# First stage of a hybrid decoder layer: all loads on one queue, the casts behind the third root, a chunk turned a quad earlier

## The chip, the core and the metric

The kernel runs on one core of a Trainium2 chip. The metric is the device time of one execution in microseconds; the median of several runs stands for a kernel. Times inside the kernel come from one profiled execution.

## The reference

One layer of a decoder trunk on 16 meta tokens and 1024 real ones, width 1024, all float32:

```
h = concat(meta, x)
h = h + 1/2 * SwiGLU_1(RMSNorm(h))          # D_FF = 2816
u = RMSNorm(h) @ W_in
o = concat[HGRN2(u), StickBreaking(u)]      # parallel head groups
h = h + o @ W_out
h = h + 1/2 * SwiGLU_2(RMSNorm(h))
return h without the meta tokens

rms_norm(x, g) = x * rsqrt(mean(x*x) + 1e-6) * g
swiglu(h, w_in, w_out): g, u = split(h @ w_in); (silu(g) * u) @ w_out
```

## The kernel before

Every matrix product is made of three matmuls with float32 operands split in a high part (a cast, `wh` or `xh`) and a rest (`wl`, `xl`): high times high, rest times high, high times rest. The high part of a weight block is cast on ScalarE (L277, ACT in the profile) and its rest subtracted on VectorE (L279, DVE). Each split pair has three buffers.

The change is in the first stage, the first product of SwiGLU_1, in `run` and `fast_in`. The 1040 tokens are split in three chunks, `THIRDS`: chunk 0 of 352 tokens, chunks 1 and 2 of 344. Each chunk is loaded as three tiles of up to 128 rows of 1024 floats (`rows_of`, `load_rows`), from HBM as it lies. `norm_rows` makes the norm of each tile: a square with a sum (L648 on ScalarE for the first and third tile, L644 on VectorE for the second), a root (L649, ScalarE), a reciprocal (L650) and a scaling of the rows (L651), both on VectorE. `turned` transposes a chunk on TensorE (L631). For chunk 0 the results are evicted with the gain and split at once into `X` (L660 on ScalarE, L661 on VectorE). For chunk 2 they become `ba` and the operands B11 and B21 (`first_block`, L673 and `halve`, L222 and L223), for chunk 1 `bb`. `first_combined` then makes the operands T2, T3, T1, T4 and B22 from `ba` and `bb` in five groups of four steps.

Chunk 0 is multiplied plainly: `plain_quad` takes four weight blocks of 128 x 512 floats (two columns blocks of 128 by two halves of the depth), 12 matmuls each, 48 in all, in bank `qd`. Six such quads (gate and up of three pairs of columns) come first; they are the work beside which chunks 2 and 1 are normed, turned and combined. Chunks 1 and 2 are then multiplied together by a scheme with seven products of half blocks in place of eight (`quad`, banks `qa`, `qb`, `qc`), in which POOL (GpSimd) makes sums of weight blocks (L292). The other columns of chunk 0 are done along with it. Raw weight blocks (`raw`, L284) are loaded on SP's queue, 256 KB each.

The order of TensorE's instructions is that of the program. The other engines and the queues are put in order by a planner, from the program's order as priority and its own estimates of time; once built, each engine works through its own order strictly. Within the first stage the program's order is: chunk 0 normed and turned (at high priority), quad 1 (`next(steps)`), chunk 2 normed, quad 2, chunk 1 normed, chunk 2 turned, quads 3 and 4, chunk 1 turned, four steps of `first_combined` and quad 5, four steps and quad 6, the other twelve steps, and the combined quads. `setup_rest` (masks and small constants for later stages, L99 to L130) stands behind the plain quads and is moved forward by the planner where an engine is free.

The loads of chunk 0 stand on SP's queue, those of chunks 2 and 1 on POOL's, which in the profile is q0 (software_dynamic); SP's is q1.

Of the kernel before, what the change touches and what calls it, by code (L numbers as in the profile page):

```python
# [11 lines left out]
F32 = mybir.dt.float32  # L12
# [3 lines left out]
AF = mybir.ActivationFunctionType  # L16
# [4 lines left out]
P = 128  # L21
D = 1024
# [12 lines left out]
def drain(gen):  # L35
    for _ in gen:
        pass


class Block:  # L40
# [221 lines left out]
    def fast_in(self, ops, n, w_in, actD, openers, ev0, open_ev, feed=None, plain=None,  # L262
# [6 lines left out]
        nc = self.nc  # L269
        wp, pin = self.wq, self.pin  # L270
# [9 lines left out]
            return hi, lo  # L280

        def block(i, h, col):
            t = wp.tile([P, 4, P], F32, tag="raw", name="raw", bufs=6)
            nc.sync.dma_start(  # L284
                t, w_in[512 * h : 512 * h + 512, col + P * i : col + P * i + P]
                .rearrange("(k p) f -> p k f", p=P)
            )
            return t
# [6 lines left out]
        def weights(col, opened, also):  # L295
            if opened:
                yield operand(block(0, 0, col))
                yield operand(block(0, 1, col))
            a11, a21, a22, a12 = (
                block(i, h, col) for i, h in ((0, 0), (1, 0), (1, 1), (0, 1))  # L300
            )
            if opened is None:
                yield operand(a11)
            s1 = made(a21, nc.gpsimd.tensor_add, a22)
            s2 = made(s1, nc.gpsimd.tensor_sub, a11)
            yield operand(s2)
            if opened is None:
                yield operand(a12)
            yield operand(made(a11, nc.gpsimd.tensor_sub, a21))
            yield operand(s1)  # L310
            yield operand(a22)
            yield operand(made(a12, nc.gpsimd.tensor_sub, s2))
            if also:
                yield operand(a21)
# [323 lines left out]
    def norm_rows(self, ci, rows, junk):  # L638

        nc = self.nc  # L640
        for i, (row, at, m) in enumerate(rows):
            s, r = self.ss[:m, 3 * ci + i, 0:1], self.ss[:m, 3 * ci + i, 1:2]
            if i == 1:
                nc.vector.scalar_tensor_tensor(  # L644
                    junk[1][:m], row[:m], 1.0, row[:m], ALU.mult, ALU.mult, accum_out=s
                )
            else:
                nc.scalar.activation(junk[0][:m], row[:m], AF.Square, accum_out=s)  # L648
            nc.scalar.activation(r, s, AF.Sqrt, bias=self.eps[:m], scale=1.0 / D)  # L649
            nc.vector.reciprocal(r, r)  # L650
            nc.vector.tensor_scalar_mul(row[:m], row[:m], r)  # L651

# [673 lines left out]
    def run(self):  # L1326
        nc, tc, a = self.nc, self.tc, self.a
# [19 lines left out]
        with ExitStack() as c0:  # L1347
            with ExitStack() as c1:
                with tc.manual_schedule(engines={nc.tensor.engine}), ExitStack() as c2:
                    xo = self.pool("x_ops", ctx=c2)  # L1350
                    plain = [xo.tile([P, KT, n0], F32R, name=f"X0{i}") for i in range(2)]
                    ops = {
                        x: [xo.tile([P, 4, nw], F32R, name=f"{x}{i}") for i in range(2)]
                        for x in names
                    }
                    self.wq = self.pool("w1", ctx=c2)
                    ev0 = self.pool("ev10", ctx=c2)
                    self.pin = self.pool("pin1", 1, PSUM, c2)
                    self.t_bufs = 2
                    c3 = ExitStack()  # L1360
                    rp = self.pool("rows", ctx=c3, side="right")
                    junk = [rp.tile([P, D], (BF16, U8)[i], name=f"junk{i}") for i in range(2)]
                    self.row_bufs = 9
                    rows = [self.rows_of(0, rp, nc.sync)]
                    rows += [self.rows_of(ci, rp, nc.gpsimd) for ci in (2, 1)]
                    turning = []

                    def open_ev():
                        self.setup_rest(rp)
                        c3.close()  # L1370
                        ev = self.pool("ev1", ctx=c2)
                        turning.append(self.turn_x(self.pool("turn", ctx=c2), xD))
                        return ev

                    def between():
                        next(turning[0], None)

                    steps = self.fast_in(
                        ops, nw, a["ffn1_w_in"][0], act1D, 3, ev0, open_ev, None, plain, between
                    )  # L1380
                    with tc.high_priority():
                        self.first_plain(rows[0], junk, plain)
                    next(steps)
                    self.norm_rows(2, rows[1], junk)
                    next(steps)
                    self.norm_rows(1, rows[2], junk)
                    ba = self.first_block(2, rows[1], rp, "ba", ops)
                    next(steps)
                    next(steps)
                    bb = self.first_block(1, rows[2], rp, "bb", None)  # L1390
                    made = self.first_combined(ba, bb, ops, rp, nw)
                    for _ in range(2):
                        for _ in range(4):
                            next(made)
                        next(steps)
                    drain(made)
                    drain(steps)
                    drain(turning[0])
# [170 lines left out]
            with tc.manual_schedule(engines={nc.tensor.engine}), ExitStack() as cx:  # L1569
                with ExitStack() as c1:  # L1570
# [58 lines left out]
                    for i in summed(1, cB):  # L1629
                        if i == 4:  # L1630
                            r = self.inv_rms_rows(sums[0], n, px, pps)
                        if i == 7:
                            r = self.spread_rows(r, n, px, pps)
# [5 lines left out]
                operands(xb, ("T2", "T3", "T1", "T4", "B22"))  # L1639
                self.wq = self.pool("wq", ctx=cx)  # L1640
                self.pin = self.pool("pin2", 1, PSUM, cx)
                self.t_bufs = 2
                ppb = self.pool("ppb", 1, PSUM, pre)

                def open_ev():
# [8 lines left out]
                steps = self.fast_in(ops, n, a["ffn2_w_in"][0], actD, 2, ev0, open_ev, made)  # L1654
                r = self.inv_rms_rows(sums[1], n, px, ppb)
# [49 lines left out]
```

## Time and profile before

| | |
|---|---|
| runs | 2135.32, 2140.38, 2140.86 us (median 2140.38) |
| the profiled execution | 2136.56 us |
| its span | 2134.9 us |
| mean granted clock of TensorE | 0.988 |
| TensorE busy (matmul) | 2049.6 us, 96% |
| VectorE, ScalarE, POOL busy | 64%, 42%, 32% |
| first product of chunk 0 | 22.40 us after the span's start |
| first combined quad | 80.34 us |

The page gives the busy time of each engine, then its share in 40 slices of the span in tenths (9 is 90% or more). In the lists in order of time a row has the start and the length in us, the engine (PE is TensorE's matmul), the line, the operation, what it writes and reads, the shapes, and in brackets how long the engine stood idle before it and who released it. Matmuls overlap in the pipeline, so their lengths add up to more than the time they take.

### The profile page before, as it was taken

The numbers are of one execution on the slowest core, as the hardware profiler recorded it, in microseconds if no ns is written. First come the engines' busy times: TensorE is split into PE (matmuls) and PEld (weight loads), VectorE is DVE, ScalarE is ACT, GpSimd is POOL, SyncE is SP. The second block draws the span as 40 slices with busy tenths as digits, with TensorE's granted clock in tenths as the row PEclk, the third lists the DMA queues.
The fourth block names the chain that finished last, engine by engine and source line by source line (L and its number), as shares of the span: only waits on it lengthen the run. The fifth ranks groups of instructions, "written<-read, shape, count | busy, mean of one in ns | idle before, by whom it ended". The sixth has DMA issues, their size and how long they took to land. (4 is left out here: it accounts for less than half of the span.)

```text
span 2134.9 us, 32078 instructions
## 1 busy us (share of the span) xinstructions
PE 2049.6 (96%) x11520; PEld 1841.8 (86%) x11520; DVE 1358.4 (64%) x2072; ACT 899.1 (42%) x1859; POOL 673.5 (32%) x732
## 2 busy tenths in 40 slices
PE   6899999999999999999999999999899999999998
PEld 6899999999999989988887878877688888878887
DVE  5775544555589843246666757658767677676774
ACT  7543333333465633455565623335223333234443
POOL 2265544452000322333443400112545454440000
PEclk9999999999999999999999999999999999999999
DMA  6543333324867735434444171334533333358363
GB/s 178 163 153 118 121 105 102 103 92 174 263 197 227 228 93 160 145 129 114 117 138 113 59 262 49 97 114 123 173 104 109 94 109 99 104 180 278 104 202 133
DMA packets 271311, 300.19 MB, mean 141 GB/s; under 512 B 24784, under 2 KB 197904, under 8 KB 271152
## 3 DMA queue, kind: packets, MB, share of 16 engines
q1 hardware_dynamic: 252656, 244.88, 38.0%
q0 software_dynamic: 17456, 53.26, 6.8%
q8 instruction: 91, 1.49, 0.3%
q14 instruction: 68, 0.56, 0.1%
q10 hardware_dynamic: 1040, 0.00, 0.0%
HBM read 215.96 MB, written 82.11 MB: 140 GB/s over the span
## 5 line engine op out<-in xcount | busy, mean ns | idle before, releaser
L320 PE MATMUL qb<-T,wh 128*128 128x344 f32 (+1 forms) x1056 | 312.4, 358 | 11.0 <-DVE u L362 7.1
L279 DVE TENSOR_TENSOR wl<-s,wh 128x512 fp32r<-128x512 f32 x176 | 203.5, 1157 | 115.1 <-ACT wh L277 112.2
L320 PEld LDWEIGHTS qb<-T,wh 128*128 128x128 f32 x1056 | 194.0, 190 | 36.0 <-ACT wh L277 8.8
L588 PE MATMUL o<-tl,wh 128*128 128x344 f32 (+1 forms) x616 | 219.2, 357 | 3.4 <-DVE tl L518 3.3
L588 PE MATMUL o<-th,wh 128*128 128x344 f32 (+1 forms) x616 | 219.2, 357 | 3.3 <-DVE hT L598 3.3
L588 PE MATMUL o<-th,wl 128*128 128x344 f32 (+1 forms) x616 | 218.9, 357 | 0.7 <-DVE wl L518 0.7
L320 PE MATMUL qa<-B,wh 128*128 128x344 f32 (+1 forms) x704 | 210.4, 363 | 0.0
L163 PE MATMUL proj<-xh,wh 128*128 128x344 f32 (+2 forms) x576 | 208.0, 361 | 0.9 <-ACT xh L1443 0.9
L277 ACT CAST wh<-s 128x512 fp32r<-128x512 f32 x176 | 109.4, 622 | 225.9 <-PE qb L320 158.3
L279 DVE TENSOR_TENSOR wl<-raw,wh 128x512 fp32r<-128x512 f32 x172 | 151.0, 881 | 81.1 <-ACT wh L277 77.5
L164 PE MATMUL proj<-xh,wl 128*128 128x344 f32 (+2 forms) x576 | 202.1, 351 | 0.0
L165 PE MATMUL proj<-xl,wh 128*128 128x344 f32 (+2 forms) x576 | 201.7, 350 | 0.2 <-POOL xl L1444 0.2
L277 ACT CAST wh<-raw 128x512 fp32r<-128x512 f32 x172 | 106.0, 620 | 200.7 <-PE qc L320 98.3
L320 PE MATMUL qb<-T,wl 128*128 128x344 f32 (+1 forms) x528 | 188.8, 358 | 0.0
L320 PE MATMUL qd<-X,wh 128*128 128x352 f32 x704 | 181.2, 325 | 0.7 <-DVE X L661 0.7
L516 ACT CAST th<-act 128x512 fp32r<-128x512 f32 (+2 forms) x176 | 95.3, 542 | 183.0 <-PE o L588 129.9
L292 POOL TENSOR_TENSOR s<-raw 128x512 f32<-128x512 f32 x88 | 120.5, 1370 | 103.7 <-DVE wl L279 69.8
L518 DVE TENSOR_TENSOR tl<-act,th 128x512 fp32r<-128x512 f32 (+2 forms) x176 | 109.9, 627 | 67.0 <-ACT th L516 66.9
L320 PEld LDWEIGHTS qa<-B,wh 128*128 128x128 f32 x704 | 129.6, 190 | 16.1
L1212 POOL TENSOR_TENSOR sig<-sig,keep 128x144 f32<-128x144 f32 (+3 forms) x64 | 92.0, 1437 | 146.2 <-DVE keep L1209 86.2
L588 PEld LDWEIGHTS o<-tl,wh 128*128 128x128 f32 x616 | 117.0, 190 | 17.1 <-DVE tl L518 4.8
L320 PE MATMUL qa<-B,wl 128*128 128x344 f32 (+1 forms) x352 | 127.0, 361 | 3.9 <-DVE wl L279 3.9
(332 smaller groups left out, 4916.8 us busy)
## 6 DMA issues: line engine op xcount, KB each, us to landing
raw<-in_ffn_w_in_dram SPq DMA_DIRECT2D x208, 256.0 KB, 3.1
raw<-in_ffn_w_out_dram SPq DMA_DIRECT2D x176, 256.0 KB, 4.0
raw<-in_w_in_dram SPq DMA_DIRECT2D x28, 512.0 KB, 4.2
ks<-kD SPq DMA_DIRECT2D x32, 260.0 KB, 5.3
ak<-in_ffn_w_out_dram SPq DMA_DIRECT2D x22, 256.0 KB, 4.6
hT<-xD SPq DMA_DIRECT2D x8, 520.0 KB, 8.7
xD<-xts POOLq DMA_DIRECT2D x16, 256.0 KB, 2.8
vD<-vhl SPq DMA_DIRECT2D x8, 512.0 KB, 4.7
```

The lines of the kernel that those rows point to most:

```text
L163: nc.tensor.matmul(ps, wh[:, s], xs, start=k == 0, stop=False)
L164: nc.tensor.matmul(ps, wl[:, s], xs, start=False, stop=False)
L165: nc.tensor.matmul(ps, wh[:, s], xl[:, k, c0 : c0 + n], start=False, stop=k == nk - 1)
L277: nc.scalar.copy(hi, src)
L279: nc.vector.tensor_sub(lo, src, hi.bitcast(F32))
L292: op(t, x, y)
L320: nc.tensor.matmul(ps, a[:, k, :], b[:, k0 + k, :], start=start and k == 0 and i == 0, stop=k == 3 and i == 2, skip_group_check=True,)
L516: nc.scalar.copy(hi, src)
L518: nc.vector.tensor_sub(lo, src, hi.bitcast(F32))
L588: nc.tensor.matmul(banks[bank][m], y[:, m * P : (m + 1) * P], z, start=start and q == 0 and e == 0, stop=q == nq - 1 and e == 2, skip_grou ...
L1212: nc.gpsimd.tensor_mul(sig, sig, keep[:, 1 : nk + 1])
```

## The change

Four edits. The rows of chunks 2 and 1 are loaded on SP's queue, and their loads are written at the place where the chunk is needed: chunk 2 behind quad 2's weights, chunk 1 behind quad 3's; chunk 1 is also normed later, behind quad 3. The instructions of quad 1 on ScalarE are put behind the root of chunk 0's third tile (`issue_after` orders instructions of that engine and adds no wait between engines). Chunk 1 is turned after the third quad in place of the fourth, and three quads in place of two stand between four steps each of `first_combined`. Raw weight blocks have eight buffers in the first stage in place of six (six as before in the second SwiGLU), and row tiles eight in place of nine.

```diff
         def block(i, h, col):
-            t = wp.tile([P, 4, P], F32, tag="raw", name="raw", bufs=6)
+            t = wp.tile([P, 4, P], F32, tag="raw", name="raw", bufs=self.in_bufs)
...
-            nc.scalar.activation(r, s, AF.Sqrt, bias=self.eps[:m], scale=1.0 / D)
+            self.root = nc.scalar.activation(
+                r, s, AF.Sqrt, bias=self.eps[:m], scale=1.0 / D
+            )
...
-                    self.t_bufs = 2
+                    self.t_bufs, self.in_bufs = 2, 8
...
-                    self.row_bufs = 9
+                    self.row_bufs = 8
                     rows = [self.rows_of(0, rp, nc.sync)]
-                    rows += [self.rows_of(ci, rp, nc.gpsimd) for ci in (2, 1)]
...
                     with tc.high_priority():
                         self.first_plain(rows[0], junk, plain)
+                    with tc.issue_after(self.root.ins):
+                        next(steps)
                     next(steps)
+                    rows.append(self.rows_of(2, rp, nc.sync))
                     self.norm_rows(2, rows[1], junk)
-                    next(steps)
-                    self.norm_rows(1, rows[2], junk)
                     ba = self.first_block(2, rows[1], rp, "ba", ops)
                     next(steps)
-                    next(steps)
+                    rows.append(self.rows_of(1, rp, nc.sync))
+                    self.norm_rows(1, rows[2], junk)
                     bb = self.first_block(1, rows[2], rp, "bb", None)
                     made = self.first_combined(ba, bb, ops, rp, nw)
-                    for _ in range(2):
+                    for _ in range(3):
                         for _ in range(4):
                             next(made)
                         next(steps)
...
-                self.t_bufs = 2
+                self.t_bufs, self.in_bufs = 2, 6
```

## The prediction

> **What bounds the kernel now.** I read the page first, then the stretches of the first 90 us, then the order of time on each engine there, and last the DMA queues. The page:
>
> ```profile
> span 2134.9 us, 32078 instructions
> PE 2049.6 (96%) x11520; PEld 1841.8 (86%) x11520; DVE 1358.4 (64%) x2072; ACT 899.1 (42%) x1859; POOL 673.5 (32%) x732
> PE   6899999999999999999999999999899999999998
> ```
>
> TensorE is busy 96% of the span, and 36 of the 40 slices stand at 9. So only what TensorE loses can be won, and what it gains early is carried to the end, because no later slice waits for anything but TensorE. The first slice (53 us) is a 6, the second an 8. The change touches these two. The stretches of them:
>
> ```profile
> 0.00:22.40 22.40, 5.19 (x24) 4.52 (x24) 7.97 (x22) 9.20 (x19) 5.54 (x14) 1.00 0.97 283
> 22.40:39.84 17.44, 17.10 (x97) 16.79 (x98) 13.89 (x41) 16.90 (x31) 4.24 (x7) 1.00 0.48 104
> 39.84:44.73 4.89, 3.40 (x26) 2.66 (x25) 4.00 (x12) 4.42 (x11) 2.27 (x5) 1.00 0.36 100
> 44.73:59.87 15.14, 15.14 (x97) 15.12 (x96) 8.69 (x18) 12.20 (x22) 1.38 (x3) 1.00 0.47 136
> 80.34:84.53 4.19, 0.48 (x3) 0.19 (x3) 4.19 (x10) 1.52 (x3) 1.02 (x3) 0.89 0.51 168
> 84.53:90.00 5.47, 5.47 (x19) 5.47 (x20) 1.84 (x3) 0.96 (x2) 0.32 (x2) 0.50 0.77 222
> ```
>
> The columns are the stretch and its length, then busy us of PE, PEld, DVE, ACT and POOL, the granted clock, the DMA share and GB/s. Until 22.40 TensorE does only the 24 transposes of the first third while the DMA engines are full (0.97). Then come two plain quads (17.44), the turning of chunk 2 (4.89), two quads (15.14, so 7.57 each), the turning of chunk 1, two quads more, and at 80.34 the first combined quad, which stops for 4.19 us and then runs at half clock. The order of time around the first product:
>
> ```profile
> 9.31 3.65 PE L631 MATMUL xps<-ident,row 128*128 128x128 f32 x16 [9.31 <-DVE ss_x L650]
> 9.88 1.06 ACT L648 ACTIVATE junk<-row 96x1024 bf16<-96x1024 f32 x1 [1.01 <-DMA row<-in_x_dram]
> 16.32 0.62 ACT L277 CAST wh<-raw 128x512 fp32r<-128x512 f32 x1 [5.29 <-DMA raw<-in_ffn_w_in_dram]
> 16.84 0.29 ACT L649 ACTIVATE ss_x<-ss_x,eps 96x1 f32<-96x1 f32 x1
> 18.75 0.69 DVE L279 TENSOR_TENSOR wl<-raw,wh 128x512 fp32r<-128x512 f32 x1 [1.02 <-ACT wh L277]
> 19.36 0.74 DVE L651 TENSOR_SCALAR row<-row,ss_x 96x1024 f32<-96x1024 f32 x1
> 19.53 1.05 ACT L648 ACTIVATE junk<-row 128x1024 bf16<-128x1024 f32 x1
> 20.16 1.54 PE L631 MATMUL xps<-ident,row 96*128 96x96 f32 x8 [7.20 <-DVE row L651]
> 20.62 3.66 ACT L660 ACTIVATE X<-xps,g 128x352 fp32r<-128x352 f32 x8
> 20.63 1.22 DVE L644 SCALAR_TENSOR_TENSOR junk<-row 128x1024 uint8<-128x1024 f32 x1
> 21.77 4.01 DVE L661 SCALAR_TENSOR_TENSOR X<-xps,g,X 128x352 fp32r<-128x352 f32 x8
> 22.40 0.66 PE L320 MATMUL qd<-X,wh 128*128 128x352 f32 x1 [0.70 <-DVE X L661]
> 25.50 0.37 PE L320 MATMUL qd<-X,wl 128*128 128x352 f32 x1
> ```
>
> The third tile of rows was squared by 11.1, but its root (L649) stands on ScalarE behind a cast (L277) that waited 5.29 us for its weights. Everything after it hangs on that root. Why the weights were late, from the DMA queues in 0:5, 5:8, 10:16 and 16:20:
>
> ```profile
> q1 hardware_dynamic: 214, 0.75, 48.9%
> ...
> q1 hardware_dynamic: 157, 0.58, 53.4%
> q0 software_dynamic: 149, 0.55, 49.9%
> ...
> q0 software_dynamic: 507, 1.74, 87.2%
> q1 hardware_dynamic: 574, 0.29, 18.9%
> ...
> q1 hardware_dynamic: 2125, 1.06, 108.6%
> ```
>
> From 10 to 16 us both queues got about as many packets through (507 and 574), but those of q0 (POOL's, the rows of chunks 2 and 1) carried 1.74 MB and those of q1 (SP's, the weights) 0.29 MB. Once q0 was empty, q1 moved 1.06 MB in 4 us.
>
> **The change part by part.** *Start.* The first third is 352 rows of 4 KB, 1.44 MB. By 5.00 q1 had moved 0.75; the two queues together moved 1.13 MB in the next 3 us, 0.377 a us. With POOL's rows gone the last 0.69 MB take 1.8 us, and the third tile is there at about 6.8 instead of 9.88. Behind it a weight block (0.262 MB) takes 0.97 us at q1's 1.06 MB in 4 us: the first at 7.8, the eighth at 14.6.
>
> ```profile
> 6.87 0.16 DVE L650 RECIPROCAL ss_x<-ss_x 128x1 f32<-128x1 f32 x1 [5.24 <-ACT ss_x L649]
> 7.31 1.23 DVE L644 SCALAR_TENSOR_TENSOR junk<-row 128x1024 uint8<-128x1024 f32 x1 [0.28 <-DMA row<-in_x_dram]
> 8.58 0.29 ACT L649 ACTIVATE ss_x<-ss_x,eps 128x1 f32<-128x1 f32 x1 [1.74 <-DVE junk L644]
> ```
>
> The second tile's square on VectorE can start at 7.03 behind the reciprocal instead of 7.31, so its root ends at about 8.6. Then the third square (1.06, and 0.19 to read its sum), and the third root at 9.8 to 10.1, with the casts behind it. The reciprocal (0.16) and the scaling (0.74) bring the transposes to about 11.1. Before, 2.24 us lay from them to the first product, with a square of chunk 2 (20.63, 1.22) ahead of the X pieces on VectorE; without it, the chain is the first eviction and its rest, about 1.6. That gives 12.7 to 13.4; I take 13.1, so **-9.3 us**. If the third tile lands as late as now, it is 14.3 (-8.1); the best is 12.8 (-9.6). The first block, in hand at about 9, is cast behind the root at 10.1 to 10.7 and subtracted (0.69) by 12.1: covered by 1 us. Were that cover gone, each us of it would cost one.
>
> *Slow first products.* The products began with 11 in the 3.1 us from 22.40 to 25.50, against 7.57 / 48 = 0.158 each later (a quad has 48): 1.35 us lost. In the changed kernel the transposes from about 9 on run into the products with gaps of under 2 us, where before 7.20 us of waiting lay between. I take **-0.5**, bounds -1.35 and 0. The Trainium skill, page "TensorE: Matmul & The Clock Gate", section "What's actually happening", has the clock raised after about 3.4 us of steady work and lowered after as long an idle window; by that rule the products would run fast from about 13 on and the term would be -1.35. The records here show the lowering (0.50 behind the stop at 80), and not how short a gap is harmless at the start.
>
> *Rows of chunks 2 and 1 on SP.* Six issues move from POOL to SP. SP is in order: three of them follow the eight weight blocks of quads one and two, which need no wait with eight buffers. At 0.377 MB a us chunk 2 (1.41 MB) is in at 14.6 + 3.7 = 18.3; it is needed normed after the second quad, 13.1 + 17.44 = 30.5. Behind it stand the third quad's blocks, which wait for buffers that the first quad's subtractions free, the fourth at about 21; then chunk 1, in at some 27. It is turned after the third quad, at 30.5 + 4.89 + 7.57 = 43.0. So both transfers are hidden, the later one by over 10 us. The eight-row limit costs one wait for a tile of the first third, free at 13: nothing. The two buffers more are paid by that row buffer less.
>
> *ScalarE in the squeezed stretch.* Here is a cost. What ScalarE did from the first eviction to the turning of chunk 1 has one quad less to lie beside:
>
> ```profile
> 20.60:59.87 39.27, 36.74 (x224) 35.38 (x223) 28.38 (x75) 35.32 (x66) 7.88 (x15) 1.00 0.49 124
> L277 ACT CAST wh<-raw 128x512 fp32r<-128x512 f32 x15 | 8.9, 621 | 2.2 <-PE qd L320 2.2
> L395 ACT ACT_TABLE_LOAD x4 | 5.1, 1283 | 0.1
> ```
>
> It was busy 35.32 of 39.27 us. A quad less takes off four casts (2.5), an activation (0.46) and a table load (1.28): 31.1 us are left for 11.6 to 43.0, 31.4 us. Nothing is spare. If the handing over idles as before (3.95 us), TensorE waits 3.7 us; if it packs, nothing. I take **+2**, bounds 0 and 3.7.
>
> *Chunk 1 turned a quad earlier.* The stop at 80.34 is VectorE's backlog from the turning of chunk 1 (busy 4.19 of 4.19 in the stretch above):
>
> ```profile
> 84.53 0.66 PE L320 MATMUL qa<-B,wl 128*128 128x344 f32 x1 [3.71 <-DVE wl L279]
> L223 DVE TENSOR_TENSOR T<-ba,T 128x344 fp32r<-128x344 f32 x8 | 6.7, 868 | 0.0
> L279 DVE TENSOR_TENSOR wl<-raw,wh 128x512 fp32r<-128x512 f32 x8 | 5.3, 685 | 0.1
> L398 DVE TENSOR_TENSOR sp<-qd,sp 128x352 f32<-128x352 f32 x3 | 1.5, 516 | 0.6 <-PE qd L320 0.6
> ```
>
> With a third quad beside it VectorE gains 7.57 us and has to do four subtractions (2.7) and a product (0.5) more: 4.3 us to spare against a wait of 3.71. The balance is close, and I leave 0.5 us of it. The slow stretch behind it, 19 products in 5.47 us where 3.0 would do, goes with it: 2.5. So 3.2 + 2.5 = **-5.7**, bounds -6.2 and 0. What is late next is the second weight block of that quad, whose two sums POOL makes first; eight buffers let their loads go earlier.
>
> *Eight weight buffers later.* In the remaining quads TensorE waits 3.1 us in all (two waits of 1.54, below). More prefetch may take them or add as much: 0, bounds -3.1 and +3.1.
>
> Sum: -9.3 - 0.5 + 2 - 5.7 = **-13.5 us**. The profiled execution took 2136.56 (span 2134.9), so 2123.1. The three runs are 2135.32, 2140.38 and 2140.86; with the profiled one they average 2138.3, which is 1.7 above it. I forecast 2123.1 + 1.7 = 2125. A measurement of this kernel tells about 0.3% from no change, 6.4 us; that is also the spread of these runs.
>
> **The rivals.** *A, ScalarE waits for chunk 2 before the X evictions.* The planner already put one square of chunk 2 there (19.53, ahead of 20.62). If it does so again, that square waits for a tile that now stands behind eight weight blocks: 14.6 + 0.52 / 0.377 = 16.0, done 17.2, first product at 18.8. Start term -3.6; sum -7.3 with no other gain at the start; 2131. For it: the order of before. Against: three casts now fill that gap. Chance 0.10.
>
> *B, the gain goes to a wait for chunk 1.* A square of chunk 1 put among the casts of quads two and three stops ScalarE, from about 21.5 to 27, and with it the casts: 5.5 us, and 2.5 more of slow clock. -13.5 + 8 gives 2133. Against: wh and wl have three buffers, some 5 us ahead. Chance 0.10.
>
> *C, slower: eight buffers bring POOL's sums onto VectorE's subtractions.* It happens once or twice now:
>
> ```profile
> 121.37 3.71 DVE L279 TENSOR_TENSOR wl<-raw,wh 128x512 fp32r<-128x512 f32 x1 [0.77 <-ACT wh L277]
> 125.66 0.40 PE L320 MATMUL qb<-T,wh 128*128 128x344 f32 x1 [1.54 <-DVE u L362]
> ```
>
> A subtraction that takes 0.69 elsewhere took 3.71, and TensorE waited 1.54 us. There are 22 quads from 80 us on. If 9 of them wait so, the gain is gone; from 13 on the kernel is slower by 0.3%; all 22 cost 34 us: 2159. Against: only 2 wait now though loads run ahead with six buffers. Chance 0.07.
>
> *D, the first weights come no earlier.* If the planner puts chunk 2's rows ahead of the weights on the one queue, the bytes before the first block are almost those of now, and the start stays: -5.7 + 2, so 2134.5. The Trainium skill, "DMA: Bandwidth & Descriptors", section "Issuing engines are not separate DMA queues", says that transfers of all engines run on the same 16 DMA engines and that a second issuer saves only issue time; read alone it promises nothing from one queue, and 2134.5 would be its time. The packets in 10:16 show that what interleaved was unequal in bytes, which is the start term. Chance 0.07.
>
> **How the numbers follow.** The forecast has the remaining 0.66. Range: all bounds favourable give -9.6 - 1.35 - 6.2 - 3.1, about -20: 2118, and I go to 2116 for the spread of the runs; upward it takes in A, B and D and ends at 2136. Outside lie C and some tails, under 0.2. Faster by over 0.3% (below 2134 against 2140.4): the forecast nearly whole (0.63), most of A, a little of B: 0.73. Within 0.3%: most of B and D, and tails: 0.19. Slower: C and a rest, 0.08.
>
> **What would show it.** Right: the third root before the first cast at about 10; first product at 12.7 to 13.4; q0 without bytes before 30 us; chunk 1 turned at 43 to 46; the first combined quad at 67 to 70 with a wait under 1 us and clock 1.00 after it. Wrong: a Square (L648) ahead of L660 that waits for a row's DMA (A); TensorE waiting on casts before 45 us (B); waits of qb on u in many quads (C); the first cast still waiting at 16 us (D).

## The result and the profile after

The changed kernel takes 2121.64 us (median of four runs, 2120.94 to 2122.61) against 2139.73 us before (four runs, 2135.32 to 2140.86): ratio 0.992, 95% interval 0.9902 to 0.9937. The profiled execution took 2122.61 us, 13.95 less than the one before; the forecast for it was 2123.1.

The page after, its first rows:

```profile
span 2120.9 us, 32084 instructions
PE 2045.6 (96%) x11520; PEld 1837.1 (87%) x11520; DVE 1358.7 (64%) x2072; ACT 900.9 (42%) x1860; POOL 677.4 (32%) x726
PE   7999999999999999989999998998999999999998
```

Nearly all stays; the first slice is a 7 and the second a 9. The same stages as shown of before, by stretches (start and length, busy us of PE, PEld, DVE, ACT, POOL, granted clock, DMA share, GB/s):

```profile
0.00:15.18 15.18, 4.93 (x24) 4.66 (x24) 7.27 (x25) 8.22 (x17) 5.44 (x10) 1.00 0.97 242
15.18:33.09 17.91, 17.43 (x97) 17.12 (x98) 14.23 (x35) 15.52 (x26) 4.25 (x8) 1.00 0.98 280
33.09:37.98 4.89, 3.39 (x26) 2.65 (x25) 4.07 (x12) 4.56 (x12) 1.76 (x5) 1.00 0.90 198
37.98:45.48 7.50, 7.50 (x49) 7.48 (x49) 4.41 (x14) 7.45 (x14) 0.00 (x0) 1.00 0.28 37
45.48:51.30 5.82, 4.17 (x25) 3.19 (x24) 3.87 (x8) 5.24 (x11) 0.00 (x0) 0.85 0.01 3
51.30:76.70 25.40, 24.26 (x146) 23.67 (x145) 24.20 (x46) 20.07 (x42) 9.81 (x5) 0.97 0.34 97
```

The start is 15.18 us long instead of 22.40, the turning of chunk 1 (fifth row) 5.82 instead of 3.90, at a clock of 0.85, and the three quads behind it 25.40, where three of 7.57 would be 22.7. The start in order of time, ScalarE, VectorE and TensorE together:

```profile
8.79 1.04 ACT L648 ACTIVATE junk<-row 96x1024 bf16<-96x1024 f32 x1
9.33 4.93 PE L631 MATMUL xps<-ident,row 128*128 128x128 f32 x24 [9.33 <-DVE ss_x L652]
9.96 0.29 ACT L649 ACTIVATE ss_x<-ss_x,eps 96x1 f32<-96x1 f32 x1
10.16 1.76 ACT L277 CAST wh<-raw 128x512 fp32r<-128x512 f32 x3
10.60 0.75 DVE L653 TENSOR_SCALAR row<-row,ss_x 96x1024 f32<-96x1024 f32 x1
13.17 3.66 ACT L662 ACTIVATE X<-xps,g 128x352 fp32r<-128x352 f32 x8 [1.25 <-PE xps L631]
14.19 0.23 DVE L121 CAST masks<-sd 128x128 uint8<-128x128 f32 x1 [1.04 <-POOL sd L117]
14.59 3.98 DVE L663 SCALAR_TENSOR_TENSOR X<-xps,g,X 128x352 fp32r<-128x352 f32 x8
15.18 0.66 PE L320 MATMUL qd<-X,wh 128*128 128x352 f32 x1 [0.93 <-DVE X L663]
```

The third root ends at 10.25, three casts run behind it without a wait, and the third tile is scaled by 11.35. All of that is as forecast. But the 16 transposes of the first two tiles go slowly (24 in 4.93 us) and let the third tile's through only by 13; and a piece of later work, the cast of a mask (L121) that waits for POOL, stands on VectorE ahead of the X pieces. The DMA queue in 10:16, where before q1 had 0.29 MB beside q0's 1.74:

```profile
q1 hardware_dynamic: 2969, 1.86, 115.5%
```

### The profile page after: what moved, and what is told of

Its sections match the earlier page's. It is cut to its first block, busy times and chain, and to the rows that moved or that the text cites. A ratio compares the mean times of both kernels' runs of the same rounds, so it can differ in the third digit from the quotient of the medians.

```text
span 2120.9 us, 32084 instructions
## 1 busy us (share of the span) xinstructions
PE 2045.6 (96%) x11520; PEld 1837.1 (87%) x11520; DVE 1358.7 (64%) x2072; ACT 900.9 (42%) x1860; POOL 677.4 (32%) x726
## 5 line engine op out<-in xcount | busy, mean ns | idle before, releaser
L292 POOL TENSOR_TENSOR s<-raw 128x512 f32<-128x512 f32 x88 | 125.4, 1425 | 94.6 <-DVE wl L279 70.0
L588 PEld LDWEIGHTS o<-th,wh 128*128 128x128 f32 x616 | 116.4, 189 | 15.6 <-ACT th L516 3.4
```

The costliest lines, as they stand in the source:

```text
L292: op(t, x, y)
L588: nc.tensor.matmul(banks[bank][m], y[:, m * P : (m + 1) * P], z, start=start and q == 0 and e == 0, stop=q == nq - 1 and e == 2, skip_grou ...
```

## The experiments

All kernels but the second traces are edits of the changed kernel. To compare their first stage I take the eviction of the last combined quad's first product there (L357): 345.79 before and 336.44 after, 9.35 earlier. The whole time also holds what varies in the later stages. Each ratio is to the kernel before, run beside that kernel; medians of different experiments are compared through these ratios.

**The casts not put behind the root.**

```diff
-                    with tc.issue_after(self.root.ins):
-                        next(steps)
+                    next(steps)
```

> The changed kernel with the first quad's casts not put behind the third root. Theory (the gain at the start is the bytes: with POOL's rows gone the first weight block is there by about 9 us): the cast that stands ahead of the root again waits for almost nothing, costs its own 0.6 us, and the first product moves from 15.2 to at most 16; 2122 to 2123. Rival (the gain at the start is the order): the root again waits for the cast and the first product is near 20 or later; 2126 to 2129.

Measured: 2123.4 us (ratio to before 0.9928, 0.9913 to 0.9943).

```profile
9.61 0.60 ACT L277 CAST wh<-raw 128x512 fp32r<-128x512 f32 x1
10.12 0.29 ACT L649 ACTIVATE ss_x<-ss_x,eps 96x1 f32<-96x1 f32 x1
14.76 0.43 PE L320 MATMUL qd<-X,wh 128*128 128x352 f32 x1 [0.65 <-DVE X L663]
```

The cast stands ahead of the root again and waits for nothing, since the block is there by 9.6. The first product is even 0.4 us earlier, the last quad at 334.49; 1.5 of these 1.95 us are products that ran at full pace from the start. The order alone earns nothing once the bytes come in time.

**The rows on POOL's queue**, all else as changed.

```diff
-                    rows.append(self.rows_of(2, rp, nc.sync))
+                    rows.append(self.rows_of(2, rp, nc.gpsimd))
-                    rows.append(self.rows_of(1, rp, nc.sync))
+                    rows.append(self.rows_of(1, rp, nc.gpsimd))
```

> The changed kernel with the rows of chunks 2 and 1 on POOL's queue, all else as changed. Theory (bytes): the weights again trickle beside the rows, the first block comes at about 16 and the first product at 17.5 to 19; 2124.5 to 2126. Rival (order): the root is free of the cast, the first product stays near 15 to 16; 2122.

Measured: 2133.59 us (0.9981, 0.997 to 0.9991), the last quad at 346.26.

```profile
11.24 0.29 ACT L649 ACTIVATE ss_x<-ss_x,eps 96x1 f32<-96x1 f32 x1
16.35 0.62 ACT L277 CAST wh<-raw 128x512 fp32r<-128x512 f32 x1 [4.82 <-DMA raw<-in_ffn_w_in_dram]
21.16 3.65 ACT L662 ACTIVATE X<-xps,g 128x352 fp32r<-128x352 f32 x8
22.62 0.66 PE L320 MATMUL qd<-X,wh 128*128 128x352 f32 x1 [8.97 <-DVE X L663]
```

The root is free at 11.24, and it does not help: the three casts stand ahead of the X evictions too, so the first product is at 22.62, as before the change. I had expected 17.5 to 19 and overlooked that second place. Both runs say that the start is the queue's doing. With this edit undone the first stage is back where it was, though chunk 1 is still turned a quad earlier: the parts do not simply add up.

**Chunk 1 turned after the fourth quad.**

```diff
+                    next(steps)
                     bb = self.first_block(1, rows[2], rp, "bb", None)
...
-                    for _ in range(3):
+                    for _ in range(2):
```

> The changed kernel with chunk 1 turned after the fourth quad as before (two quads between the steps of first_combined). Theory (VectorE's backlog): the first combined quad stops again for 3 to 4 us and runs slow behind it, 5 to 6 us, while the turning of chunk 1 takes 3.9 instead of 5.8 us and keeps its clock, 3 us back: 2124 to 2125. Rival (the stop went because chunk 1's loads and norms moved, not its turning): no stop, 2118 to 2121.

Measured: 2130.36 us (0.9959, 0.9945 to 0.9973), the last quad at 342.03. Neither came out as a whole: the stop at the first combined quad is gone, as the rival has it (0.24 us are left), but the time is lost earlier, in the plain quads:

```profile
83.42 0.43 PE L320 MATMUL qa<-B,wl 128*128 128x344 f32 x1 [0.24 <-DVE wl L279]
48.58 0.42 PE L320 MATMUL qd<-X,wh 128*128 128x352 f32 x1 [1.64 <-ACT wh L277]
```

By stretches, the two quads before the turning and the two behind it:

```profile
38.30:58.52 20.22, 18.28 (x97) 17.74 (x97) 9.15 (x20) 14.62 (x26) 0.55 (x1) 0.87 0.33 86
62.66:82.90 20.24, 17.65 (x97) 16.75 (x96) 20.05 (x38) 14.49 (x31) 4.82 (x4) 0.92 0.33 92
```

The two quads before the turning take 20.22 us and the two behind it 20.24, against 15.14 and 16.57 in the kernel before. TensorE waits for casts and for weight halves, 4.6 us in all, and the granted clock is 0.87 and 0.92. VectorE's backlog (20.05 of 20.24 us) is there as I said, but it is paid in the plain quads; ahead of the turning VectorE is not full (9.15 of 20.22), and the wait shown is for ScalarE. So in this trace the kernel that turns a quad earlier is 5.6 us ahead. By my estimate about 1.7 of that is luck: the clock stood at 0.50 from 36.68 to 40.09, 3.41 us, a fall that began in the turning of chunk 2, which the edit does not touch. That the earlier turning works by taking away the stop at 80 is not shown, since the stop is gone without it.

**Six raw buffers.**

```diff
-                    self.t_bufs, self.in_bufs = 2, 8
+                    self.t_bufs, self.in_bufs = 2, 6
```

> The changed kernel with six raw weight buffers. Theory (the second quad's last two blocks and chunk 2's rows then wait behind the first quad's subtractions, still early enough): within 1 us, 2121 to 2123. Rival (two buffers more are what feeds the first quads): TensorE waits for weight halves before 45 us, 2124 or more.

Measured: 2125.81 us (0.9938, 0.9923 to 0.9952); the interval overlaps that of the changed kernel. The last quad is at 337.51, 1.1 us later. One wait comes back at the change of stage (TensorE's waits, 505 to 545; columns us in total, times, longest):

```profile
PE o L554 <- ACT wh L516: 0.7, 1, 0.7
```

It stands in all three traces with six buffers (0.8 us in both of before, with 0.3 us behind it for the rest), and in none of the eleven with eight. There the shift between the traces of before and after grows from 9.36 to 11.01 us.

**Both kernels once more, for a second trace.**

> The kernel before, unchanged, for a second trace. Of the 14.0 us between the two traces 9.4 are gained by 90 us and 4.7 come in small steps from 530 us on, where the granted clock of a stretch fell in one trace and not in the other. Theory (chance, where a pause falls against the clock's windows): the same steps come elsewhere or not at all in this trace, some us either way, while everything up to 500 us repeats within 0.3 us. Rival (the changed order of work later on): the steps repeat in the same places.

> The changed kernel again, for a second trace. Chance: up to 500 us as in the first trace within 0.3 us, later stretches off by some us. Order: all the same within 0.5 us.

Measured: 2137.4 us (span 2135.7) and 2121.99 us (span 2120.3). The stretch 40:50 of before, first trace and then second:

```profile
40.00:50.00 10.00, 8.51 (x58) 7.77 (x57) 8.24 (x22) 9.49 (x22) 3.10 (x7) 1.00 0.34 97
```

```profile
40.00:50.00 10.00, 8.50 (x49) 7.74 (x48) 8.29 (x25) 9.41 (x21) 3.31 (x8) 0.83 0.38 115
```

The same instructions, the same waits, and in the second trace the clock fell in the turning of chunk 2:

```profile
44.99:48.40 3.41, 3.41 (x17) 3.41 (x16) 2.86 (x10) 3.41 (x9) 1.17 (x3) 0.50 0.36 101
```

That cost it 1.6 us, in the turning (5.38 instead of 4.89) and the two quads behind it (16.24 instead of 15.14). Another 0.8 us were lost before, since the first products stayed slow for longer (first two quads 18.28 instead of 17.44). Its last quad is at 348.22, 2.4 us later, though I had expected 0.3 us. The changed kernel repeated within 0.5 (335.97). So the first stage's gain is 9.4 to 12.2 us over the four pairs of traces. What lies behind it gains 3.0 to 4.8 us in each pair; 1.65 of that is the wait at the change of stage. The rest comes in steps of about 0.3 to 1.7 us in both directions, several of them where a clock falls in one trace and not in another, and two traces of one kernel differ by such steps too (1.6 us in sum for the kernel before). The other experiments tell against a steady gain of this size: from the last quad to the end of the span the kernels with the casts not ordered, with POOL's queue and with the late turning take 1787.8, 1787.7 and 1789.2 us, as long as the kernel before (1789.1 and 1787.5), though they too have eight buffers and no wait at the change of stage; the changed kernel takes 1784.5 and 1784.3. Over all traces this part takes 1779.6 to 1789.2 us with eight buffers (eleven) and 1787.5 to 1789.1 with six (three). So it varies from execution to execution by more than the gain; how much of the gain belongs to the change stays open.

**TensorE at work while it waits: products, or transposes, of the identity.**

```diff
+                    hot = self.pin.tile([P, P], F32, tag="qa", name="hot", bufs=2)
+                    for _ in range(20):
+                        nc.tensor.matmul(hot, self.ident, self.ident, start=True, stop=True)
                     with tc.high_priority():
                         self.first_plain(rows[0], junk, plain)
```

The second kernel has 36 of `nc.tensor.transpose(hot, self.ident, self.ident)` there.

> The changed kernel with 20 products of the identity with itself on TensorE from about 1.5 us on, while it waits for the first rows; their result is not used. Theory (transposes do not raise the clock, products do; that is why 4.9 us of transposes were followed by slow products): the clock is up by 9 us, the 24 transposes take about 2.5 to 3 instead of 4.9 us, the first products run at 0.16 us each, first product at 13 to 14; 2118 to 2120. Rival (the records' slow pace at the start is something else, such as the first use of the weights): first product and pace as before the edit, 2121 to 2123.

> The same with 36 transposes of the identity in place of the 20 products. Theory (transposes do not count for the clock): no gain, slow transposes and slow first products as in the changed kernel; 2121 to 2123. Rival (any work of TensorE counts and the changed kernel's 24 transposes were too few): as with the products, 2118 to 2120.

Measured: 2127.57 us (0.9948, 0.993 to 0.9965) and 2128.24 us (0.9946, 0.9925 to 0.9966), both medians above that of the changed kernel, with intervals that just overlap its own. The first, TensorE and VectorE:

```profile
9.03 1.97 PE L631 MATMUL xps<-ident,row 128*128 128x128 f32 x16 [0.87 <-DVE row L653]
11.15 0.88 PE L631 MATMUL xps<-ident,row 96*128 96x96 f32 x8 [0.15 <-DVE row L653]
18.79 0.23 DVE L121 CAST masks<-sd 128x128 uint8<-128x128 f32 x1 [0.85 <-POOL sd L117]
19.19 3.98 DVE L663 SCALAR_TENSOR_TENSOR X<-xps,g,X 128x352 fp32r<-128x352 f32 x8
19.78 0.66 PE L320 MATMUL qd<-X,wh 128*128 128x352 f32 x1 [7.75 <-DVE X L663]
```

The second, TensorE:

```profile
1.49 7.04 PE L1384 MATMUL hot<-ident 128*128 128x128 f32 x36 [1.49 <-POOL ident L68]
9.30 1.97 PE L631 MATMUL xps<-ident,row 128*128 128x128 f32 x16 [0.76 <-DVE row L653]
```

Two things follow. Transposes raise the clock as products do: in both, 16 transposes take 1.97 us where 16 took 3.65 before the change. My theory on that fell. The 24 transposes of the changed kernel are at the edge of what is needed: the products behind them began slow in both its traces (15.18 and 15.03) and at full pace in the runs with six buffers and with the late turning (15.21 and 15.32), where the 24 took 4.2 instead of 4.9 us. (In these two the granted clock then stood at 0.50 for 3.41 us from about 16.2, so their first two quads were little faster: 17.3 and 17.4 instead of 17.9 us.) And the gain was lost again, because four rounds of masks now stood ahead of the X pieces; that the planner put them there because TensorE was longer at work is my guess.

**The masks behind the X pieces**, alone and with the products.

```diff
-            nc.vector.scalar_tensor_tensor(lo, ps, g, hi.bitcast(F32), ALU.mult, ALU.subtract)
+            self.last_x = nc.vector.scalar_tensor_tensor(
+                lo, ps, g, hi.bitcast(F32), ALU.mult, ALU.subtract
+            )
...
-                        self.setup_rest(rp)
+                        with tc.issue_after(self.last_x.ins):
+                            self.setup_rest(rp)
```

> The changed kernel with VectorE's part of setup_rest put behind the last X piece. In the run with products of the identity, four rounds of masks (each a VectorE write, two POOL steps and a VectorE cast, 1.6 us) stood ahead of the X pieces and held the first product to 19.8 though the third tile was turned by 12.0; in the changed kernel one round stood there, with 1.04 us of waiting. Theory (this is the second of the two things that kept the start from 13.1, beside the slow transposes): first product about 1 us earlier, 14.0 to 14.3; 2120 to 2122. Rival (X waits for something else then): first product at 15.

> As the last, and 20 products of the identity on TensorE from 1.5 us on. Theory (transposes at the slow pace cost 2 us of the start and slow first products 1.4): transposes done by 12.1, first product at 12.5 to 13.2 and at full pace, so 3 to 4 us ahead of the changed kernel at the first combined quads; 2117 to 2119. Rival (the time goes to ScalarE's queue before chunk 1 is turned): first product at 13, but the turning of chunk 1 starts no earlier than 44 and the end gains under 1.5 us.

Measured: 2117.53 us for the masks alone (0.9914, 0.9899 to 0.9929; 2116.82 to 2120.3) and 2124.66 with the products (0.994, 0.9918 to 0.9961). The first product of each:

```profile
13.95 0.43 PE L320 MATMUL qd<-X,wh 128*128 128x352 f32 x1 [0.53 <-DVE X L663]
```

```profile
13.60 0.43 PE L320 MATMUL qd<-X,wh 128*128 128x352 f32 x1 [1.42 <-DVE X L663]
```

The two quads behind it in the second of them, with the products:

```profile
13.60:32.49 18.89, 17.21 (x97) 16.90 (x98) 13.01 (x32) 15.76 (x26) 3.53 (x6) 0.91 1.00 262
```

The masks were the second thing that kept the start from 13.1: without them it is 13.95, and the last quad is at 333.43, 3.0 us earlier than in the changed kernel. It is the fastest kernel of all tried, but its interval overlaps that of the changed kernel, and of the 3.0 us only 1.2 are the start. The rest came behind it, in a trace in which the clock was up at 13.95 and did not fall in this stage. With the products the rival holds, in what it said of the time: the start is 0.35 us earlier still, the turning of chunk 1 starts at 46.73, and the last quad is at 336.16, 0.3 us ahead of the changed kernel. The first two quads take 18.89 us instead of 17.40 with the masks alone:

```profile
13.95:31.35 17.40, 15.64 (x97) 15.33 (x98) 13.86 (x35) 16.23 (x28) 4.36 (x7) 1.00 1.04 295
```

Both wait once for a weight half there (1.7 and 1.8 us), and the DMA engines are full in both (1.00 and 1.04). The difference is the clock, which stood at 0.50 from 14.59 to 18.00 behind the 1.42 us of waiting for X.

**Chunk 1 normed ahead of chunk 2's turning, and chunk 1's squares on VectorE**, both on top of the masks. The first moves `rows_of(1, ...)` and `norm_rows(1, ...)` two lines up, ahead of `ba = ...`; the second is

```diff
-            if i == 1:
+            if i == 1 or ci == 1:
```

> As the first of these, with chunk 1 loaded and normed (in program order) ahead of the turning of chunk 2. Theory (the turning of chunk 1 takes 5.8 instead of 3.9 us because the root of its third tile comes late, between two Silu and two table loads): it takes 3.9 to 4.1, the clock stays up behind it, 2 to 3 us gained over the run with the masks alone; 2117 to 2120. Rival (ScalarE is full before it, and what is normed earlier is paid by casts later): the quads ahead of it take as much longer, no gain, 2120 to 2122.

> The changed kernel with the masks behind the X pieces, and all three squares of chunk 1 on VectorE (two of them stood on ScalarE, 1.25 us each with the reading of the sum). Theory (ScalarE, busy 9.9 of 10 us from 40 to 50, sets how long the turning of chunk 1 takes): ScalarE is rid of 2.5 us, the turning starts and ends earlier, takes 4 to 5 instead of 5.3 us, and the first combined quad comes 1.5 to 2.5 us earlier than with the masks alone; 2115 to 2117. Rival (VectorE, full from 50 us on, becomes the bound): the quads behind the turning take longer by what is won, 2117 to 2119.

Measured: 2123.26 us (0.9944, 0.9927 to 0.9961) and 2123.72 us (0.9934, 0.9918 to 0.995), the last quads at 334.99 and 338.77. The turning of chunk 2 and the quad behind it in the first, and a wait and a stretch of the second:

```profile
30.80:37.40 6.60, 3.94 (x27) 2.96 (x24) 5.84 (x17) 4.92 (x13) 4.17 (x5) 0.92 0.71 122
37.40:46.89 9.49, 9.11 (x51) 8.80 (x50) 7.24 (x24) 8.17 (x15) 2.57 (x6) 0.87 0.31 85
```

```profile
28.93 0.66 PE L320 MATMUL qd<-X,wl 128*128 128x352 f32 x1 [3.47 <-DVE wl L279]
```

```profile
30.00:40.00 10.00, 8.50 (x49) 7.75 (x49) 8.79 (x21) 6.12 (x15) 1.83 (x3) 0.84 0.77 169
```

What is moved out of one place stalls another. In the first, the turning of chunk 2 takes 6.60 us and the clock falls. In the second, ScalarE has room (6.12 of 10), TensorE waits 3.47 us for a weight half, and the next ten us run at 0.84. Neither shortens the time to the first combined quad (76.1 and 80.0, against 73.6 with the masks alone). Both theories fell: ScalarE is not the only bound of this stretch, VectorE and the clock bound it too.

## Why the prediction was right, and where its steps were not

The forecast of 2125 and the -13.5 us of its sum came out (2121.64; -14.0 by the spans), but partly by luck. The terms of the first stage, for which there was a mechanism, gave 9.4 us in place of 13.5; 4.7 us from the later stages, put at nothing, made up for it. By term, in the first pair of traces:

| term | forecast | measured |
|---|---|---|
| start, to the first product | -9.3 | -7.2 |
| slow first products, first two quads | -0.5 | +0.5 |
| squeezed stretch, turning of chunk 1 and plain quads | +2 | +3.1 |
| first combined quads | -5.7 | -5.7 |
| later | 0 | -4.7 |

Of the signs that were named, the third root ahead of the first cast (9.96), q0 without bytes, the turning of chunk 1 (45.48) and the wait and clock of the first combined quad came out. The first product (15.18) and the first combined quad (76.70, not 67 to 70) did not. The second sign was also lower than its own sum: 80.34 - 9.3 - 0.5 + 2 is 72.5. And a block of 0.262 MB at 1.06 MB in 4 us takes 0.99 us, not 0.97; nothing hangs on that.

*Start.* The mechanism was right up to the scaled third tile: bytes, third tile's square at 8.8, root at 10, weights in hand. The mis-sized term is what lies from the scaled tile to the first product. I let the transposes of the third tile follow at 11.1, though the row of before already showed 16 transposes taking 3.65 us; and I named the square of chunk 2 on VectorE, but not that the planner could put other work there. The mask did 1.04 us of harm, and the run with the masks behind the X pieces gives it back.

*Slow first products.* No gain: the products came to full pace at about 18.6 in the changed kernel (two of them took 0.79 us before and 0.48 after). That this is the clock is read from the pace alone, for the profile's column stands at 1.00 at the start of every trace, slow products or not. The Trainium skill, "TensorE: Matmul & The Clock Gate", section "What's actually happening", says that the activity window runs freely and is not reset when a kernel starts, so that the point of rising differs from run to run with where the first matmul falls in it. The traces agree that it differs: the pace at the first product, at about 15.2, was slow in two and full in two others.

*Squeezed stretch.* ScalarE was full (9.91 of 10 us from 40 to 50), as worked out. The turning of chunk 1 took 1.9 us more. About 1.1 of that is waiting, since the root of its third tile stands between two Silu activations with their table loads:

```profile
42.73 1.28 ACT L395 ACT_TABLE_LOAD   x1
44.50 1.28 ACT L649 ACT_TABLE_LOAD   x1
46.11 1.28 ACT L395 ACT_TABLE_LOAD   x1
```

The other 0.8 of the turning is its last twelve transposes, which took 3.23 instead of 2.38 us as the clock fell. The remaining 1.2 us, net in the plain quads, I had not priced: the clock stood at 0.50 from 49.51 to 52.92, into the products behind the turning. (The wait of 1.05 us for a weight half is no loss against before, which had one of 0.98.) With the masks behind the X pieces, where the clock did not fall, the same stretch is 1.8 us longer than before, close to the +2.

*First combined quads.* The wait is 0.67 instead of 3.71 us and the clock stays at 1.00:

```profile
77.85 0.43 PE L320 MATMUL qa<-B,wl 128*128 128x344 f32 x1 [0.67 <-DVE wl L279]
```

To the first eviction this gives 4.6 us, to the second 1.1 more: the forecast 5.7. The count of VectorE's work with one more quad beside it (0.5 us of wait left) was good to 0.2 us. So the number of this term came out, but its mechanism is only half shown: with the late turning the stop is gone too, and the backlog is paid in the plain quads.

*Later.* I looked for the effect of eight buffers in the combined quads, where the shift does not change from 94 us to 520, and it came at the next stage's first loads instead. The rest of this term (some 3 us) is not explained; that it filled what the first stage fell short is luck.

*The rivals.* A did not happen in the changed kernel, but something like it did: work of lower need ahead of X, on VectorE rather than ScalarE. B did not happen: ScalarE waits for no row of chunk 1, and the 1.1 us beyond the +2 have the other sources told above. C did not: TensorE's waits of qb on u are 5.8 us in all after the change, and were 7.1 before. D is refuted by q1's 1.86 MB in 10:16.

## What to carry to other kernels

When a first load is late, look at the packets of each queue in that stretch: a second queue with larger packets can take most of the bytes while the packet counts look equal, and putting the loads on one queue in the order of need can then do what an order on the engines does not; here the order alone gained nothing. Before pricing an earlier start, follow every instruction that stands between the freed one and the first product on each engine, work of later stages included, since a planner moves it into just those gaps. In a stage whose engines are all near full, moving work from one to another mostly moves the wait, and each wait of TensorE can cost slow products besides.

## What the runs showed of the hardware

- Rows in packets of 4 KB and weights in packets of 512 bytes on two queues went through at almost the same count of packets (507 and 574 in 6 us), so the bytes were shared 6 to 1.
- Pauses of the same length lower TensorE's clock in one execution and not in the next: with two pauses of 0.41 and 0.87 us, the turning of chunk 2 in the kernel before ran on at 1.00 in one trace, and in the other the clock stood at 0.50 from 44.99 to 48.40, which cost about 1.6 us. The falls named in this text last 3.41 us each.
- Transposes raise the clock like products, by the pace: after 7.0 us of transposes 16 more took 1.97 us, as after 6.7 us of products, against 3.65 us without either.
